# Gated linear attention with 26 of its projection tiles computed in pairs, by seven products of quarters, and with x kept in DRAM meanwhile

## Chip, cores and metric

The kernel runs on one core of one Trainium2 chip, in one launch. The metric is the device time of a run in microseconds (us). Before the change the median of 3 runs is 1719.75 us (1718.37 to 1721.04).

## What is computed

The program is a whole model on 512 tokens with 1024 channels: a first block (convolution, attention, feed-forward), and a second with a layer of gated linear attention and one of sparse attention. Only the gated-attention layer changes:

```python
def gla_mixer(x, w_in, w_a2, b_a, gn_g, w_out):
    h = x @ w_in                              # q, k, v, z, a side by side
    ...
    g = jax.nn.log_sigmoid((a @ w_a2 + b_a).astype(jnp.float32)) / GLA_GATE_NORM
    ...
    q_t = q * (GLA_DK ** -0.5) * jnp.exp(G)
    k_t = k * jnp.exp(-G)
    ...
    o = o * lax.rsqrt(jnp.mean(o * o, axis=-1, keepdims=True) + NORM_EPS)
    o = o.reshape(B, L, D_INNER) * gn_g
    return (o.astype(x.dtype) * jax.nn.silu(z)) @ w_out
...
x = layer_norm(ALPHA * x + y, ln_g[i], ln_b[i])
```

There are 4 heads. Of each, queries and keys are 2 x 256 channels and the gate z has 512, so q, k and z together are 8 tiles of 128 channels a head, each of them 1024 x 128 weights times x.

## The kernel before

All tensors are held with channels on the 128 partitions and the 512 tokens along the free axis. Precision comes from splitting: a float32 operand is held as a high and a low part (`XH`, `XL` for x, `whi`, `wlo` for weights), and a product of two is three matmuls (high times high, high times low, low times high). `split` makes them: a copy on ACT (the high part), then a subtraction on DVE (the low part). Every call of an engine through a helper is recorded on L112.

One projection tile (`proj` and `part`, L237 to L252) loads 1024 x 128 weights by one DMA on SP's queue (`slab`, a `raw` buffer of 4), splits them in two halves of 128 x 512 (8 buffers of `whi` and 8 of `wlo`), and runs 8 steps of three 512-column matmuls, 24 in all, into one PSUM bank (`bank("mm")`, three of them in turn). Then the bank is read once: a copy to `gqk` for a tile of queries or keys (`gla_qk`), Silu to `gz` for a gate (`gla_z`), both on ACT.

The main loop (L1310 to L1362) goes over the heads h. Ahead of it stand the decay, the scaling and `gla_v` (values) of head 0. In a head PE's order is: four steps of scores (`gla_scores`, L1266), four z tiles among them, four steps of weighted values (`gla_av`, with `weighted` at L487 and L489), the decay of the next head (`gla_decay`: two matmuls of 256 columns, then on ACT Abs, exp and Ln with a load of the function table ahead of a change of function, and on DVE `gs`), the four tiles of queries and keys of the next head, the norm (`gla_norm`: DVE multiplies `gz` by the norm that PE spread into `ps_t`, L396, and splits the result), the eight output tiles of the head (`w_out`: DVE adds each to `X`), with the exponentials of the next head (`gla_exp`), and the values of the next head (`gla_v`).

PE's order is that of the program, by hand. ACT, DVE, POOL and SP each run one queue in the order in which a scheduler placed them; weight loads and splits are placed ahead of their use (`AHEAD`). Each queue runs in order: an instruction that waits holds all behind it.

Of the kernel before, what the change touches and what calls it, by code (L numbers as in the profile page):

```python
# [92 lines left out]
def program(tc, a, out, upto=99):  # L93
# [107 lines left out]
    class Folded:  # L201
# [20 lines left out]
        def part(self, ps, xs, k0, k1, cs):  # L222
            n = len(xs)
            for k in range(k0, k1):
# [68 lines left out]
    X = cp.tile([128, DC, S], F32, name="X")  # L293
# [310 lines left out]
    for c in range(DC):  # L604
        acc.add_square(X[:, c, :])

    pos1, T1 = tmp("pos1"), sp.tile([128, S], F32, name="T1", bufs=1)
    dve.tensor_copy(pos1, posi)
    angles(T1, pos1, 0)

# [494 lines left out]

    WO = {}

    def w_out(name, grp, i, ts, sums=None, cs=FULL):
# [51 lines left out]
    jp = gq.tile([128, 128], F32, name="jp")  # L1160
# [84 lines left out]
    def gla_z(h, i):  # L1245
# [59 lines left out]
    gla_z(0, 0)  # L1305
    for b in range(NB):
        gla_v(0, b, (lambda: None, lambda: gla_exp(0, 0), lambda: gla_exp(0, 1), lambda: None)[b])
    gla_z(0, 1)
    for h in range(4):
        gla_scores(h, 0)  # L1310
# [450 lines left out]
```

## Time and profile before

| | |
|---|---|
| median of 3 runs | 1719.75 us (1718.37 to 1721.04) |
| profiled execution: time, span | 1719.7 us, 1718.0 us |
| PE busy | 1704.8 us, 99% of the span |
| DVE, ACT, POOL busy | 1197.1, 870.9, 70.3 us (70%, 51%, 4%) |
| mean granted TensorE clock | 0.998 |
| the gated-attention layer | about 812 to 1195 us of the span |

"Busy" counts the time in which an engine has an instruction under way. A matmul's row gives its start and a length; matmuls overlap, so what one costs is read from the distance of two starts. "idle before" names who ended the idle time ahead of an instruction. The granted clock is that of TensorE, 1.00 being 2.4 GHz and 0.50 being 1.2 GHz.

### The profile page before, as it was taken

Reading aid. Unit: us, or ns where it says so; the run is one execution under the profiler, and the core shown is the slowest. Engines: PE = TensorE matmul, PEld = TensorE weight load, DVE = VectorE, ACT = ScalarE, POOL = GpSimd, SP = SyncE. Lnnn points to the kernel's source line nnn. Section 1 sums busy time; section 2 is a strip of 40 time slices with the busy share of each in tenths; the row PEclk is TensorE's granted clock in tenths of the full one; section 3 lists DMA queues with packets and bytes.
Section 4 is the critical chain, followed back from the end, with each engine's and each line's share of the span. In section 5 each row is a group of like instructions: output and inputs, shape, how many; then the busy total and the mean of one; then the engine's idle time right before and its main releaser. Section 6 shows DMA issues by size and latency. Waiting matters only on the chain.

```text
span 1718.0 us, 23818 instructions
## 1 busy us (share of the span) xinstructions
PE 1704.8 (99%) x8815; PEld 1453.1 (85%) x8815; DVE 1197.1 (70%) x2604; ACT 870.9 (51%) x1642; POOL 70.3 (4%) x98
## 2 busy tenths in 40 slices
PE   9999999999999999999999999999999999999999
PEld 7788888898888888899888888888988888888898
DVE  8788545389727657688545473546879987888886
ACT  7466433365434434455753644533765356444554
POOL 2244000000000000000000000000000000000000
PEclk9999999999999999999999999999999999999999
DMA  6232332223333232333312322224232232121231
GB/s 217 86 99 74 123 98 98 86 76 111 96 98 95 80 115 85 98 123 125 104 60 70 102 83 86 74 86 135 85 125 74 87 98 62 62 75 62 68 105 62
DMA packets 51188, 161.11 MB, mean 94 GB/s; under 512 B 6144, under 2 KB 7552, under 8 KB 51072
## 3 DMA queue, kind: packets, MB, share of 16 engines
q1 hardware_dynamic: 49968, 157.82, 28.7%
q0 software_dynamic: 960, 1.57, 0.4%
q8 instruction: 69, 1.13, 0.3%
q14 instruction: 47, 0.39, 0.1%
q10 hardware_dynamic: 144, 0.20, 0.0%
HBM read 153.28 MB, written 4.72 MB: 92 GB/s over the span
## 4 chain that ended last, share of the span: by engine, by line
PE 94%; DVE 3%; ACT 2%; issue 1%; DMA 0%; POOL 0%; SPq 0%; ACTq 0%; DVEq 0%
PE ps_mm L246 71%; PE ps_s L246 7%; PE ps_o L487 2%; PE ps_mm L273 2%; PE ps_mm L274 2%; PE ps_mm L272 2%; PE ps_t L505 1%; PE ps_s L272 1%; PE ps_t L1266 1%; PE ps_s L274 1%; PE ps_s L273 1%; PE ps_t L396 1%; PE ps_s L487 1%; DVE wlo L112 0%; PE ps_s L1204 0%
## 5 line engine op out<-in xcount | busy, mean ns | idle before, releaser
L112 ACT ACTIVATE whi<-raw 128x512 fp32r<-128x512 f32 (+1 forms) x550 | 336.8, 621 | 433.8 <-PE ps_mm L246 375.9
L246 PE MATMUL ps_mm<-XH,wlo 128*128 128x512 f32 (+1 forms) x1381 | 516.9, 374 | 0.3 <-DVE up L112 0.3
L246 PE MATMUL ps_mm<-XH,whi 128*128 128x512 f32 (+1 forms) x1381 | 515.3, 373 | 0.0
L246 PE MATMUL ps_mm<-XL,whi 128*128 128x512 f32 (+1 forms) x1381 | 514.6, 373 | 0.0
L112 DVE TENSOR_TENSOR wlo<-raw,whi 128x512 fp32r<-128x512 f32 (+2 forms) x547 | 368.1, 683 | 167.0 <-ACT whi L112 165.1
L246 PEld LDWEIGHTS ps_mm<-XH,wlo 128*128 128x128 f32 x1381 | 260.4, 189 | 45.7 <-DVE wlo L112 0.8
L246 PEld LDWEIGHTS ps_mm<-XL,whi 128*128 128x128 f32 x1381 | 260.4, 189 | 45.7 <-DVE XL L112 0.2
L246 PEld LDWEIGHTS ps_mm<-XH,whi 128*128 128x128 f32 x1381 | 260.6, 189 | 44.0 <-ACT whi L112 0.4
L112 DVE SCALAR_TENSOR_TENSOR upt<-up,vec,upt 128x511 f32<-128x511 f32 (+1 forms) x88 | 65.4, 750 | 10.7 <-ACT upt L112 9.5
L112 ACT ACT_TABLE_LOAD x47 | 60.3, 1283 | 6.8 <-issue 2.1
L246 PE MATMUL ps_mm<-fh,wlo 128*128 128x512 f32 (+1 forms) x153 | 55.7, 364 | 0.0
L246 PE MATMUL ps_mm<-fl,whi 128*128 128x512 f32 (+1 forms) x153 | 55.6, 363 | 0.0
L246 PE MATMUL ps_mm<-fh,whi 128*128 128x512 f32 (+1 forms) x153 | 55.6, 363 | 0.0
L272 PE MATMUL ps_mm<-whi,XH 128*128 128x512 f32 x128 | 50.2, 392 | 0.4 <-ACT whi L112 0.4
L273 PE MATMUL ps_mm<-wlo,XH 128*128 128x512 f32 x128 | 50.0, 390 | 0.3 <-DVE wlo L112 0.3
L274 PE MATMUL ps_mm<-whi,XL 128*128 128x512 f32 x128 | 49.9, 390 | 0.0
L246 PE MATMUL ps_mm<-pthi,wlo 128*128 128x512 f32 (+1 forms) x128 | 48.7, 381 | 0.0
L112 DVE TENSOR_TENSOR up<-ps_mm,RU 128x512 f32<-128x512 f32 x41 | 28.2, 691 | 29.0 <-PE ps_mm L246 29.0
L246 PE MATMUL ps_mm<-ptlo,whi 128*128 128x512 f32 (+1 forms) x128 | 48.0, 375 | 0.4 <-DVE ptlo L112 0.2
L246 PE MATMUL ps_mm<-dth,wlo 128*128 128x512 f32 (+1 forms) x128 | 48.1, 376 | 0.0
L246 PE MATMUL ps_s<-XL,whi 128*128 128x256 f32 (+1 forms) x160 | 47.5, 297 | 0.6 <-DVE XL L112 0.6
L246 PE MATMUL ps_mm<-dtl,whi 128*128 128x512 f32 (+1 forms) x128 | 48.1, 375 | 0.0
(546 smaller groups left out, 3163.0 us busy)
## 6 DMA issues: line engine op xcount, KB each, us to landing
raw<-in_w_ffn_up SPq DMA_DIRECT2D x44, 512.0 KB, 3.5
raw<-in_dsa_w SPq DMA_DIRECT2D x38, 512.0 KB, 3.5
raw<-in_w_in SPq DMA_DIRECT2D x31, 512.0 KB, 3.3
raw<-in_gla_qk SPq DMA_DIRECT2D x16, 512.0 KB, 4.1
raw<-in_gla_z SPq DMA_DIRECT2D x16, 512.0 KB, 3.5
raw<-in_gla_v SPq DMA_DIRECT2D x16, 512.0 KB, 3.4
raw<-in_gla_w_out SPq DMA_DIRECT2D x16, 512.0 KB, 3.5
raw<-in_ple_gate_w SPq DMA_DIRECT2D x16, 512.0 KB, 3.5
```

The costliest lines, as they stand in the source:

```text
L112: r = f(*args, **kw).ins
L246: pe.matmul(ps[:m, cs], l_, r_, start=(k == 0 and i == 0), stop=(k == n - 1 and i == 2))
L272: pe.matmul(ps, lh, rh, start=(i == 0), stop=False)
L273: pe.matmul(ps, lh, rl, start=False, stop=False)
L274: pe.matmul(ps, ll, rh, start=False, stop=(i == n - 1))
L396: pe.matmul(ps[:, b * 128:(b + 1) * 128], r.to_broadcast([128, 128]), ident, start=True, stop=True)
L487: pe.matmul(ps[:m, c0:], vs[j][a_], r[b_], start=(j == 0 and i == 0), stop=(j == NB - 1 and i == 2))
L505: pe.transpose(ps[:, j * 128:(j + 1) * 128], p_[:, j * 128:(j + 1) * 128], ident)
L1266: pe.matmul(ps_[:, bi], l_, r_, start=(c == 0), stop=(c == 1))
```

## The change

Two tiles of 128 channels become one `Pair`. Its weights are a 2 x 2 block: a, b the two halves of the first tile's 1024 rows, c, d those of the second; x is a 2 x 2 block too (its lower and upper 512 channels, by the first and the last 256 tokens). Seven products of quarters replace eight. POOL makes four sums of the weights' quarters (128 x 512 each); seven parts are split on ACT and DVE instead of four. A product is 4 steps of three 256-column matmuls, so a pair has 84 of 256 columns where two tiles had 48 of 512. The seven accumulate into halves of two banks b0 and b1 of "mm": products 0, 2 and 4 into the first half of b0 (each on top of the one before), product 1 into its second half; 3 and 6 into the first half of b1, 5 into its second half. After products 0, 2 and 4 ACT copies the half bank to `kept`; after 1, 4, 5 and 6 DVE adds a half bank and a half of `kept` to the output.

Thirteen pairs are made: the first two z tiles of heads 1 to 3, the last two z tiles of all four heads, and both pairs of queries and keys of heads 1 to 3. `x_forms` makes the four sums of x's quarters once, in `gla_v` of head 0: 8 operations on POOL, 8 copies on ACT, 8 subtractions on DVE (`TH`, and `XT`, which takes `X`'s place). `X` is stored to DRAM (`XD`, eight DMAs of 256 KB); the output tiles of heads 0 to 2 inside the loop load their x tile into `xio` (two buffers), add, and store it; at head 3 x comes back by eight loads. `X` becomes tiles of two chunks (class `Chunks`, left out below); `gs` has one buffer instead of two.

```diff
+    class Pair:
+        def __init__(self, ap0, ap1):
...
+            (a_, b_), (c_, d_) = ((t_[:, :S], t_[:, S:]) for t_ in raw)
+            self.todo, self.parts = [a_, b_, a_, c_, tmp("s1"), b_, d_], []
+            with tc.high_priority(offset=AHEAD):
+                gps.tensor_tensor(self.todo[4], c_, d_, op=OP.add)
+                self.split(2)
+                gps.tensor_tensor(c_, a_, c_, op=OP.subtract)
+                gps.tensor_tensor(a_, self.todo[4], a_, op=OP.subtract)
+                gps.tensor_tensor(b_, b_, a_, op=OP.subtract)
...
+            def product(n):
+                if n == 0:
+                    st["b"] = bank("mm"), bank("mm")
+                b0, b1 = st["b"]
+                self.split(1)
+                ps = (b0[:, lo_], b0[:, hi_], b0[:, lo_], b1[:, lo_], b0[:, lo_], b1[:, hi_], b1[:, lo_])[n]
+                hi, lo = self.parts[n]
+                xs_ = quarters[n]
+                for k in range(4):
+                    th, tl = xs_[k]
+                    kc = slice(k * 128, k * 128 + 128)
+                    for i, (l_, r_) in enumerate(((hi, th), (hi, tl), (lo, th))):
+                        pe.matmul(ps, l_[:, kc], r_, start=(n in (0, 3) and k == 0 and i == 0),
+                                  stop=(k == 3 and i == 2), skip_group_check=n not in (0, 3))
...
+                if n in (0, 2, 4):
+                    copy(k1 if n == 2 else k0, ps, scale=scale)
+                if n == 1:
+                    sum_(o0[:, lo_], ps, k0)
+                elif n == 4:
+                    sum_(o1[:, hi_], b1[:, lo_], k0)
+                elif n == 5:
+                    sum_(o0[:, hi_], ps, k0)
+                elif n == 6:
+                    sum_(o1[:, lo_], ps, k1)
+                    done()
...
+        if away:
+            x_ = gp.tile([128, S], F32, name="xio", tag="xio", bufs=2)
+            with tc.high_priority(offset=AHEAD):
+                nc.sync.dma_start(x_, away[i])
...
+        if away:
+            nc.sync.dma_start(away[i], x_)
...
+    def gla_z_pair(h, i):
...
+        return Stream(pair.steps(x_quarters(), (two[:, 0, :], two[:, 1, :]), kept,
+                                 done=lambda: act.activation(two, two, AF.Silu)))
...
         gla_scores(h, 1)
         if h:
-            gla_z(h, 0)
+            z01.run(4)
         gla_scores(h, 2)
         gla_scores(h, 3)
+        z23 = gla_z_pair(h, 2)
         if h:
-            gla_z(h, 1)
+            z01.drain()
         if h < 3:
             gla_decay(h + 1, 0)
-        gla_z(h, 2)
+        z23.run(4)
+        if h < 3:
+            qk01 = gla_qk_pair(h + 1, 0)
         gla_av(h, 0)
-        gla_z(h, 3)
+        z23.drain()
...
             gla_av(h, 2)
-            gla_qk(h + 1, 0)
+            qk01.run(4)
+            qk23 = gla_qk_pair(h + 1, 2)
             gla_av(h, 3)
-            gla_qk(h + 1, 1)
+            qk01.drain()
             r = rms(GACC[h], 512, LN_EPS, "rg")
-            gla_qk(h + 1, 2)
+            qk23.run(4)
             gla_norm(h, spread(r))
-            gla_qk(h + 1, 3)
+            qk23.drain()
```

So the loop runs products 0 to 3 of a pair, then a step of other work (scores, weighted values, the spread of the norm), then products 4 to 6.

The compiled orders show how the parts stand to each other. First PE, at the turn from the second to the third z tile of head 1, with the decay between them (`W`, `AS`); before:

```order
L246 MATMUL ps_mm<-XH,whi 128x512
L246 MATMUL ps_mm<-XL,whi 128x512
L1178 MATMUL ps_s<-W_7609,AS 128x256 [waits PE_49]
L1178 MATMUL ps_s<-W_7609,AS 128x256
L246 MATMUL ps_mm<-XH,wlo 128x512 [waits DVE_49,Activation_49]
L246 MATMUL ps_mm<-XH,whi 128x512
```

After the change, on PE, the end of product 4 and the start of product 5 of that head's first z pair:

```order
L278 MATMUL ps_mm<-TH,whi 128x256
L278 MATMUL ps_mm<-XT_7898,whi 128x256
L278 MATMUL ps_mm<-TH,wlo 128x256
L278 MATMUL ps_mm<-XH,whi 128x256 [waits DVE_49]
L278 MATMUL ps_mm<-XL,whi 128x256
L278 MATMUL ps_mm<-XH,wlo 128x256
```

A tile had its waits (for its bank and its split weights) at its first matmuls. In a pair, product 1 waits for ACT's copy of product 0, product 2 for DVE's sum of product 1, product 4 for the copy of product 2, product 5 for DVE's sum behind product 4 (here), and product 6 for DVE's sum of product 5. The waits hold a bank as a whole, although the halves differ.

Next ACT, at the same turn: the end of z's first pair and the start of the second. `ge` is the decay's Abs, exp and Ln. Before, in head 0:

```order
L112 ACTIVATE ge<-ge 128x512 [waits Activation_49]
L112 ACTIVATE whi<-raw 128x512 [waits DMAHW0_49,PE_49]
L112 ACT_TABLE_LOAD
L112 ACTIVATE ge<-ge 128x512 [waits Activation_49]
L112 ACT_TABLE_LOAD
L112 ACTIVATE gz<-ps_mm 128x512 [waits PE_49]
```

And after the change, on ACT, at that turn in head 1:

```order
L112 ACTIVATE whi<-raw 128x512 [waits PE_49]
L112 ACTIVATE ge<-ps_s 128x512 [waits PE_49]
L112 ACT_TABLE_LOAD
L112 ACTIVATE gz<-gz 128x1024 [waits DVE_49]
L112 ACT_TABLE_LOAD
L112 ACTIVATE ge<-ge 128x512 [waits Activation_49]
L112 ACTIVATE kept<-ps_mm 128x256 [waits PE_49]
L112 ACT_TABLE_LOAD
L112 ACTIVATE ge<-ge 128x512 [waits Activation_49]
```

The copy to `kept` behind product 0 of the second pair stands behind the decay's Abs, Silu of both tiles of the first pair, two loads of the table and the decay's exp; a third load and Ln follow it.

Last DVE, at the norm of a head, among the products of the second pair of queries and keys. Before:

```order
L112 TENSOR_TENSOR gz<-ps_t,gz 128x512 [waits PE_49]
L112 TENSOR_TENSOR gz<-ps_t,gz 128x512 x2
L112 TENSOR_TENSOR ptlo<-gz,pthi 128x512 [waits Activation_49] x3
L112 TENSOR_TENSOR gz<-ps_t,gz 128x512
L112 TENSOR_TENSOR wlo<-raw,whi 128x512
```

And after the change, on DVE, there:

```order
L112 TENSOR_TENSOR gz<-ps_t,gz 128x512 [waits PE_49]
L112 TENSOR_TENSOR gz<-ps_t,gz 128x512 x2
L112 TENSOR_TENSOR ptlo<-gz,pthi 128x512 [waits Activation_49] x2
L112 TENSOR_TENSOR gz<-ps_t,gz 128x512
L112 TENSOR_TENSOR ptlo<-gz,pthi 128x512 [waits Activation_49]
L112 SCALAR_TENSOR_TENSOR gqk<-ps_mm,kept 128x256
L112 TENSOR_TENSOR ptlo<-gz,pthi 128x512 [waits Activation_49]
```

The sum behind product 4, for which product 5 waits, stands behind seven operations of the norm; before, nothing that PE's next matmuls needed stood there.

## Rows read from the trace of the kernel before

**Rows 1.** The page, part 4: the chain that ended last, by engine.

```profile
PE 94%; DVE 3%; ACT 2%; issue 1%; DMA 0%; POOL 0%; SPq 0%; ACTq 0%; DVEq 0%
```

**Rows 2.** Busy time by engine and granted clock, the gated-attention layer.

```profile
812.00:1195.00 383.00, 381.71 (x1870) 321.05 (x1869) 203.93 (x407) 192.16 (x303) 0.96 (x3) 1.00 0.27 87
```

**Rows 3.** Timeline of PE (start, length): first and last matmul of a z tile.

```profile
848.32 0.39 PE L246 MATMUL ps_mm<-XH,wlo 128*128 128x512 f32 x1
...
853.53 0.40 PE L246 MATMUL ps_mm<-XL,whi 128*128 128x512 f32 x1
```

**Rows 4.** Timeline of PE: 256-column matmuls, first and last of 24.

```profile
798.60 0.28 PE L246 MATMUL ps_mm<-XH,wlo 128*128 128x256 f32 x1
...
801.36 0.28 PE L246 MATMUL ps_mm<-XL,whi 128*128 128x256 f32 x1
```

**Rows 5.** Timeline of all engines: a split that PE waits for.

```profile
828.00 0.61 ACT L112 ACTIVATE whi<-raw 128x512 fp32r<-128x512 f32 x1
...
828.67 0.50 PE L272 MATMUL ps_mm<-whi,XH 128*128 128x512 f32 x1 [0.37 <-ACT whi L112]
...
828.74 0.68 DVE L112 TENSOR_TENSOR wlo<-raw,whi 128x512 fp32r<-128x512 f32 x1
...
829.48 0.50 PE L273 MATMUL ps_mm<-wlo,XH 128*128 128x512 f32 x1 [0.30 <-DVE wlo L112]
...
829.82 0.40 PE L274 MATMUL ps_mm<-whi,XL 128*128 128x512 f32 x1
```

**Rows 6.** Timeline: scores end on PE, DVE reads them.

```profile
832.83 1.05 PE L1204 MATMUL ps_s<-dec,gs 128*128 128x128 f32 x8
...
833.92 0.17 DVE L112 COPY ends<-ps_s 128x8 f32<-128x8 f32 x1 [2.18 <-PE ps_s L1204]
```

**Rows 7.** Groups by shape, ACT, whole run (busy us, mean ns).

```profile
L112 ACT ACTIVATE whi<-raw 128x512 fp32r<-128x512 f32 x513 | 318.6, 630 | 400.6 <-PE ps_mm L246 348.3 <-PE ps_s L246 23.7 <-issue 20.8
L112 ACT ACT_TABLE_LOAD x47 | 60.3, 1283 | 6.8 <-issue 2.1 <-PE ps_s L246 1.6 <-PEq L1752 1.2
...
L112 ACT ACTIVATE pthi<-ps_t 128x256 fp32r<-128x256 f32 x28 | 10.6, 377 | 0.2 <-PE ps_t L505 0.2
...
L112 ACT ACTIVATE ex<-ex 128x1024 f32<-128x1024 f32 x8 | 8.4, 1050 | 0.0
```

**Rows 8.** Groups by shape, DVE, whole run.

```profile
L112 DVE TENSOR_TENSOR wlo<-raw,whi 128x512 fp32r<-128x512 f32 x513 | 350.1, 692 | 165.4 <-ACT whi L112 163.5
...
L112 DVE SCALAR_TENSOR_TENSOR pn<-Ee,vec,ps_t 128x256 f32<-128x256 f32 x16 | 7.6, 475 | 0.0
```

**Rows 9.** Timeline of DVE: the norm of head 0 (`gla_norm`).

```profile
895.21 1.89 DVE L112 TENSOR_TENSOR gz<-ps_t,gz 128x512 f32<-128x512 f32 x3 [2.25 <-PE ps_t L396]
897.01 1.89 DVE L112 TENSOR_TENSOR ptlo<-gz,pthi 128x512 fp32r<-128x512 f32 x3
898.81 0.69 DVE L112 TENSOR_TENSOR gz<-ps_t,gz 128x512 f32<-128x512 f32 x1
```

**Rows 10.** Busy time by engine and granted clock, around an idle PE.

```profile
79.00:80.00 1.00, 0.00 (x0) 0.00 (x0) 0.31 (x2) 0.66 (x2) 0.91 (x2) 1.00 0.62 239
...
82.00:83.00 1.00, 1.00 (x6) 1.00 (x6) 0.31 (x2) 0.61 (x2) 0.95 (x1) 0.50 0.30 98
```

**Rows 11.** Timeline of PE there: the idle time, and 512-column matmuls behind it.

```profile
81.01 0.66 PE L505 MATMUL ps_t<-con,p 128*128 128x128 f32 x2 [2.65 <-ACT p L112]
...
82.75 0.63 PE L246 MATMUL ps_mm<-XH,whi 128*128 128x512 f32 x1
83.17 0.63 PE L246 MATMUL ps_mm<-XL,whi 128*128 128x512 f32 x1
```

**Rows 12.** Timeline of POOL and of DVE: one sum each, at one time.

```profile
67.61 1.61 POOL L695 TENSOR_TENSOR ac<-ac,rub 128x512 f32<-128x512 f32 x1 [7.81 <-DVE ac L112]
...
67.97 2.40 DVE L112 TENSOR_TENSOR wlo<-raw,whi 128x512 fp32r<-128x512 f32 x2
```

**Rows 13.** The page, part 6: issue to landing.

```profile
Ee<-e2d SPq DMA_DIRECT2D x7, 256.0 KB, 4.7
```

More of the change, by code (lines that the diff above doesn't have):

```diff
@@ L229, in part, with split, steps, sum_ @@
                     pe.matmul(o_, w_, x_[:, cs], start=(k == 0 and i == 0), stop=(k == n - 1 and i == 1))
+    class Pair:
+        def __init__(self, ap0, ap1):
+            with tc.high_priority(offset=AHEAD):
+                raw = []
+                for ap in (ap0, ap1):
+                    raw.append(wp.tile([128, 1024], F32, name="raw", tag="raw", bufs=4))
+                    nc.sync.dma_start(raw[-1], ap)
+            (a_, b_), (c_, d_) = ((t_[:, :S], t_[:, S:]) for t_ in raw)
[6 more added lines that the diff above has]
+                gps.tensor_tensor(b_, b_, a_, op=OP.subtract)
+        def split(self, n):
+            for _ in range(n if len(self.parts) < 7 else 0):
+                with tc.high_priority(offset=AHEAD):
+                    hi = wp.tile([128, 512], F32R, name="whi", tag="whi", bufs=WBUFS)
+                    lo = wp.tile([128, 512], F32R, name="wlo", tag="wlo", bufs=WBUFS)
+                    split(hi, lo, self.todo[len(self.parts)])
+                    self.parts.append((hi, lo))
+        def steps(self, quarters, outs, kept, scale=1.0, done=lambda: None):
+            st = {}
+            o0, o1 = outs
+            lo_, hi_ = HALVES
+            def product(n):
[12 more added lines that the diff above has]
+                                  stop=(k == 3 and i == 2), skip_group_check=n not in (0, 3))
+                def sum_(o_, ps_, kept_):
+                    dve.scalar_tensor_tensor(o_, ps_, scale, kept_, op0=OP.mult, op1=OP.add)
+                k0, k1 = kept[:, lo_], kept[:, hi_]
+                if n in (0, 2, 4):
[9 more added lines that the diff above has]
+                    done()
+            return [lambda n=n: product(n) for n in range(7)]
@@ L292, in program, with __init__, __getitem__ @@
     xin, w_in = a["xT"], a["w_in"]
-    X = cp.tile([128, DC, S], F32, name="X")
+    class Chunks:
+        def __init__(self, name, dt=F32):
+            self.name, self.dt, self.tiles = name, dt, {}
+        def __getitem__(self, at):
+            p_, c, cs = at
+            c0, n = (c.start, c.stop - c.start) if isinstance(c, slice) else (c, 1)
+            i = c0 // 2
+            if i not in self.tiles:
+                self.tiles[i] = cp.tile([128, 2, S], self.dt, name=f"{self.name}{i}", tag=f"X{i}", bufs=1)
+            return self.tiles[i][p_, slice(c0 % 2, c0 % 2 + n) if isinstance(c, slice) else c % 2, cs]
+    X = Chunks("X")
     g_first = cp.tile([128, DC], F32, name="g_first")
@@ L605, in program @@
         acc.add_square(X[:, c, :])
-    pos1, T1 = tmp("pos1"), sp.tile([128, S], F32, name="T1", bufs=1)
+    pos1, T1 = tmp("pos1"), ap_.tile([128, S], F32, name="T1")
     dve.tensor_copy(pos1, posi)
@@ L1106, in program, with w_out @@
     WO = {}
-    def w_out(name, grp, i, ts, sums=None, cs=FULL):
+    def w_out(name, grp, i, ts, sums=None, cs=FULL, away=None):
         key = name, 4 * grp + i // 2
@@ L1169, in program, with x_forms, form, quarter @@
     GS, EX, VS, ZS, PTS, TS, QKS, GACC, VW = ({} for _ in range(9))
+    XT = Chunks("XT", F32R)
+    XD = [drp.tile([128, S], F32, name=f"xd{i}", bufs=1) for i in range(DC)]
+    for i in range(DC):
+        nc.sync.dma_start(XD[i], X[:, i, :])
+    TH = gq.tile([128, 4, 4, 256], F32R, name="TH")
+    kept = gq.tile([128, S], F32, name="kept")
+    def x_forms(p):
+        two = lambda x: x.rearrange("p (a b) -> p a b", b=256)
+        b11, b12, b21, b22 = (X[:, 4 * i + 2 * p:4 * i + 2 * p + 2, cs] for i in range(2) for cs in HALVES)
+        ts = [tmp("form") for _ in range(4)]
+        t1, t2, t3, t4 = (two(t_[:, :]) for t_ in ts)
+        gps.tensor_tensor(t1, b12, b11, op=OP.subtract)
+        gps.tensor_tensor(t2, b22, t1, op=OP.subtract)
+        gps.tensor_tensor(t3, b22, b12, op=OP.subtract)
+        gps.tensor_tensor(t4, b21, t2, op=OP.subtract)
+        for f, t_ in enumerate(ts):
+            hi = TH[:, f, 2 * p:2 * p + 2, :]
+            copy(hi, two(t_[:, :]))
+            sub(two(XT[:, (0, 1, 4, 5)[f] + 2 * p, :]), two(t_[:, :]), f32v(hi))
+    def form(f):
+        return [(TH[:, f, k, :], XT[:, (0, 1, 4, 5)[f] + k // 2 * 2, k % 2 * 256:k % 2 * 256 + 256])
+                for k in range(4)]
+    def quarter(i, cs):
+        return [(XH[:, 4 * i + k, cs], XL[:, 4 * i + k, cs]) for k in range(4)]
+    def x_quarters():
+        return (quarter(0, HALVES[0]), quarter(1, HALVES[0]), form(1), form(2), form(0), quarter(1, HALVES[1]),
+                form(3))
     def gla_decay(h, i):
         if i == 0:
-            GS[h] = ga.tile([128, NB, 256], F32, name="gs", tag="gs", bufs=2)
+            GS[h] = ga.tile([128, NB, 256], F32, name="gs", tag="gs", bufs=1)
         ps_, e_ = bank("s"), tmp("ge")
@@ L1249, in gla_z, with gla_qk_pair @@
         act.activation(ZS[h][:, i, :], ps_, AF.Silu)
+    def gla_z_pair(h, i):
+        if i == 0:
+            ZS[h] = gp.tile([128, 4, S], F32, name="gz", tag="gz")
+        pair = Pair(a["gla_z"][4 * h + i], a["gla_z"][4 * h + i + 1])
+        two = ZS[h][:, i:i + 2, :]
+        return Stream(pair.steps(x_quarters(), (two[:, 0, :], two[:, 1, :]), kept,
+                                 done=lambda: act.activation(two, two, AF.Silu)))
+    def gla_qk_pair(h, j):
+        pair = Pair(a["gla_qk"][4 * h + j], a["gla_qk"][4 * h + j + 1])
+        for i in (j, j + 1):
+            QKS[h, i] = ga.tile([128, S], F32, name="gqk", tag="gqk", bufs=4)
+        return Stream(pair.steps(x_quarters(), (QKS[h, j], QKS[h, j + 1]), kept, 1.0 / 16 if j < 2 else 1.0))
     def gla_scores(h, j):
```

17 lines of the change are left out of this document (13 added, 4 removed).

## The prediction

> **What bounds the kernel now.** I read the chain that ended last first: 94% of it is PE [rows 1]. Then the windows: in the gated-attention layer (812 to 1195 us) PE is busy for 381.71 of 383 us at a granted clock of 1.00, while ACT has 192.16 us of work and DVE 203.93 us [rows 2]. So PE never waits to speak of, and the reader should see two things: time saved on PE is saved in the end, and so is time in which PE is made to stand still. The other engines have about half of the layer free, so what they do costs nothing by its sum. It costs only where PE stands until one of them has finished. The question is therefore not how many columns a pair has but what each product waits for.
>
> **What the pairs save.** From the first to the last matmul of a z tile are 23 starts in 853.53 - 848.32 = 5.21 us [rows 3], 0.2267 us for 512 columns. Matmuls of 256 columns start (801.36 - 798.60) / 23 = 0.120 us apart [rows 4]. A pair took 48 x 0.2267 = 10.88 us and takes 84 x 0.120 = 10.08 us: **-0.80 us**, and 13 x 0.80 = -10.4 us for all. Half the columns cost 0.53 of the time, so the seven eighths of the columns become 0.93 of the time.
>
> **What each product waits for.** By the compiled order, four times in a pair PE needs a result that can only begin when its own last matmul is out. The prices:
> - A 256-column matmul lasts 0.28 us where the next would start after 0.12 [rows 4]: 0.16 us until the product is in the bank.
> - A step from engine to engine: 0.04 us from PE to DVE (832.83 + 1.05 to 833.92) [rows 6], 0.06 us from ACT to PE (828.00 + 0.61 to 828.67) and from DVE to PE (828.74 + 0.68 to 829.48) [rows 5]. From PE to ACT and from ACT to DVE I take 0.03.
> - ACT's copy of 128x256 out of PSUM 0.38 us [rows 7]; DVE's sum of that shape with a factor 0.475 us [rows 8].
> - The first matmul after an idle time: the next starts 829.82 - 829.48 = 0.34 us later instead of 0.227 [rows 5], so 0.1 us each.
>
> With ACT and DVE free, PE stands for 0.16 + 0.03 + 0.38 + 0.06 = 0.63 us ahead of product 1; 0.16 + 0.04 + 0.475 + 0.06 = 0.74, and 0.1 for the start, 0.84 ahead of products 2 and 6; 0.16 + 0.03 + 0.38 + 0.03 + 0.475 + 0.06 = 1.13 ahead of product 5, whose sum needs a copy first. Product 4's wait has other work of PE in front and costs nothing; product 3 has none. Together 0.63 + 2 x 0.84 + 1.13 = 3.44 us, and with the slow starts not yet counted 3.6, so a pair costs at least 3.6 - 0.8 = **+2.8 us**, and 13 of them +36 us.
>
> **What stands in front of those copies and sums.** ACT and DVE run in order, so I add what the orders show ahead of each:
> - A split ahead of the copy behind product 0. It waits for a weight buffer that product 0 itself reads, so it cannot begin earlier: 0.62 us on ACT [rows 7]. This holds for the first z pair and the second pair of queries and keys: 0.63 + 0.62 = 1.25.
> - A split around product 4, freed by product 4 too: copy 0.62, then 0.03, DVE's subtraction 0.69 [rows 8], the sum 0.475 and 0.06: 1.87 instead of 1.13. This holds for all but one kind below.
> - The decay's chain on ACT ahead of the second z pair's first copy. After the first pair's product 6: a split (until 0.73 us), Abs 0.6, a table load 1.28, Silu of 128x1024 1.05, a table load 1.28, exp 0.63, the copy 0.38, the step 0.06, by rows of the same shapes [rows 7]: about 6.05 us, in which PE has the decay and product 0, 0.24 + 1.44 = 1.68 us. PE stands for 4.4 us. Then come a table load, Ln, `gs` (0.69), a subtraction (0.6) and the sum ahead of product 2, 3.7 us against 1.55: 2.15. In heads 1 and 2 a second z pair thus costs 4.4 + 2.15 + 1.87 + 0.84 - 0.8 = +8.4.
> - Head 0 has no Silu before it: 1.7 for the first wait, +5.8. Head 3 has no decay but the Silu: 2.1, then 0.84, 1.87, 0.84, less 0.8: +4.8.
> - The first pair of queries and keys has the second decay ahead of product 1 in the same way, with the Silu long over: 1.7 + 2.15 + 1.87 + 0.84 - 0.8 = +5.8.
> - The second has the norm on DVE ahead of the sum of product 4. From the first multiplication to the fourth's end it took 899.50 - 895.21 = 4.3 us [rows 9], and one more subtraction and the sum come after; from that 5.3 to 5.4 us, product 4 covers 1.44: 4.0. So 1.25 + 0.84 + 4.0 + 0.84 - 0.8 = +6.1.
> - The first z pair: 1.25 + 0.84 + 1.87 + 0.84 - 0.8 = +4.0.
>
> Sum: 3 x 4.0 + 2 x 8.4 + 5.8 + 4.8 + 3 x 5.8 + 3 x 6.1 = **+75 us**.
>
> **The rest.** `x_forms` gives DVE 8 x 0.69 = 5.5 us and ACT 8 x 0.62 = 5 us in `gla_v` of head 0, where both are half idle [rows 2]: 0, at most 5.5. The 20 output tiles of heads 0 to 2 that go by DRAM wait for loads of 256 KB, of which one took 4.7 us to land [rows 13], with two `xio` in turn; DVE holds only the bank's release, and three banks and the following 22 us of values give slack: 0, at most one such latency a head, 3 x 4.7 = 14. The eight loads at head 3 are issued ahead of two steps of values: 0, at most 4.7. One buffer of `gs` makes a decay wait for the exponentials of a head before, which end long ahead: 0. POOL's 52 sums run ahead with the weight loads.
>
> A subtraction on DVE that ran beside a sum on POOL did not proceed: two took 2.40 us [rows 12], where three took 1.89 [rows 9], so 1.1 us were lost while POOL worked until 69.22. The Trainium skill, SBUF — State Buffer, section "SBUF: two separate sides", calls the shared port an exclusive lock: of a DVE operation with two SBUF inputs and a GpSimd one, the loser blocks for the whole instruction. By that rule each of a pair's four sums can hold a split that stands in the path, and the trace agrees with its 2.40 us. In the sum by rows I take one such loss in every third pair, 13 / 3 x 1.1 = +5 at most, +2 taken.
>
> A pause also slows PE. After 2.65 us of idling the next 512-column matmuls started 83.17 - 82.75 = 0.42 us apart [rows 11], and the granted clock was 0.50 there, 1.2 GHz, after 1.00 before [rows 10]. From 81.01 to 83.80 at least, 2.8 us, PE ran at half speed: 1.4 us lost. Only two second z pairs and three second pairs of queries and keys have pauses of 4 us; in the former the following wait covers most. I take 3 x 1.4 = +4.
>
> **Sum:** 1719.7 (the profiled execution, the median's 1719.75) + 75 + 2 + 4 = about **1800 us**.
>
> **Rivals.**
> 1. Only the least waits (chance 0.13): splits, decay and norm finish earlier than their place tells, since every pause of PE gives ACT and DVE time. For it speaks their half-empty layer [rows 2]; against it that the splits are freed by the very product whose result is waited for, and that Silu needs the sum of product 6. 1719.7 + 36 = 1756, with half of the extras 1775.
> 2. The clock stays low (0.17): pauses of 1.9 and 2.2 us throttle too, since a pair's pauses follow each other at 1.5 to 3 us. One loss of 1.4 us a pair gives 1800 - 4 + 13 x 1.4 = 1814; two give 1832. The Trainium skill, TensorE: Matmul & The Clock Gate, section "HAM oscillation — how this bites in real kernels", tells of a kernel in which every burst behind a wait starts cold. By that rule the case of two losses a pair holds, 1832; the trace has one such place [rows 10], and it agrees.
> 3. The waits do not bite (0.04): PE streams through the products as through two tiles, because copies and sums of a half bank end beside the next half's matmuls. Then -10.4 and the time is 1709. It decides if the four pauses in a pair together stay below 0.80 us, 0.2 us each. Against it: the shortest copy alone takes 0.38 us [rows 7], and the orders show the waits.
> 4. The way of x by DRAM costs its bound of 14 (0.03), because the output tiles' additions hold their banks until a load has landed: 1814. Against it: SP has 22 us of values between two heads in which it only fetches weights.
>
> **How the numbers follow.** The forecast itself (1785 to 1808) has 0.62, rivals 1 to 4 what stands there. The range goes from the least waits, 1757, to two clock losses a pair and POOL's bound, 1832 + 3 = 1835. A measurement of this kernel tells 0.2%, 3.4 us, from no change. Faster is rival 3 with 0.04; the same needs stalls that by chance equal the gain, 0.01; slower 0.95.
>
> **What would show it.** In the profile after, the stretch of the layer is 455 to 475 us instead of 383, with PE busy for about 385 us of it. The waits of PE name ACT's `kept` (most of it, 13 x about 2) and DVE's sums on L278; the longest, about 4 us, are the second z pairs' of heads 1 and 2, and those behind the norm. 84 matmuls of a pair that start 0.12 us apart show the gain. The rest of the program keeps its time. The prediction is wrong if the sum of PE's waits on L278 is under 30 us, or if the time is lost in `w_out` behind DMAs, or in rows of 0.21 us for 256 columns at a clock of 0.50.

## The result, and the profile after

The changed kernel takes 1823.9 us (median of 6 runs, 1820.68 to 1825.19) against 1719.5 us: a ratio of 1.0604, 95% interval 1.059 to 1.0618. Its profiled span is 1822.2 us, 104.2 us longer than before. The forecast was 1800 us in a range of 1757 to 1835: the sign and the mechanism of the waits held, and the time is 24 us above.

The windows, cut ahead of the layer and behind it (columns: stretch and its length, then busy us and count of PE, PE's weight loads, DVE, ACT, POOL, then the granted clock, DMA share, GB/s):

```profile
0.00:812.00 812.00, 805.30 (x4091) 681.21 (x4092) 554.01 (x1063) 398.81 (x735) 69.94 (x92) 1.00 0.34 107
812.00:1300.00 488.00, 408.09 (x2339) 359.30 (x2338) 273.81 (x510) 222.13 (x371) 83.36 (x61) 0.94 0.29 94
1300.00:1822.00 522.00, 516.91 (x2856) 450.38 (x2854) 439.76 (x1132) 280.30 (x605) 2.77 (x5) 1.00 0.26 82
```

All of it is in the layer: about 488 us where 383 stood [rows 2]. PE stands idle for 80 of them, and is also busy for 26 us more (408 us; the forecast had said about 385). Most of that second part was not forecast. The waits of PE (us in total, times, longest) tell what ended the idle part:

```profile
PE ps_mm L278 <- ACT kept L112: 26.9, 13, 4.0
PE ps_mm L278 <- DVE gqk L112: 26.4, 18, 3.6
PE ps_mm L278 <- DVE gz L112: 20.8, 21, 1.7
PE ps_mm L314 <- DVE wlo L112: 3.7, 1, 3.7
```

The first three are the 13 x 4 = 52 waits inside pairs: 74.1 us. The fourth is one wait in head 0, which will matter below. Where before PE ran through two z tiles without a break [rows 3], a pair now reads like this one, the first z pair of head 1 (timeline of all engines: start, length; in brackets the idle time before and who ended it):

```profile
978.23 1.68 POOL L248 TENSOR_TENSOR raw<-s,raw 128x512 f32<-128x512 f32 x1 [3.04 <-DVE wlo L112]
...
979.35 0.71 DVE L112 TENSOR_TENSOR ptlo<-diag,pthi 128x128 fp32r<-128x128 f32 x1 [0.38 <-ACT pthi L112]
...
979.63 0.28 PE L278 MATMUL ps_mm<-XH,wlo 128*128 128x256 f32 x1
979.98 0.55 DVE L112 TENSOR_TENSOR ptlo<-ps_t,pthi 128x384 fp32r<-128x384 f32 x1
...
980.45 0.29 DVE L112 COPY_PREDICATED diag<-upper,ps_t 128x128 f32<-128x128 uint32 x1
980.77 0.31 ACT L112 ACTIVATE pthi<-diag 128x128 fp32r<-128x128 f32 x1 [1.07 <-DVE diag L112]
...
981.25 0.62 ACT L112 ACTIVATE whi<-raw 128x512 fp32r<-128x512 f32 x1
...
981.76 0.37 ACT L112 ACTIVATE kept<-ps_mm 128x256 f32<-128x256 f32 x1
...
982.19 0.58 PE L278 MATMUL ps_mm<-XH,whi 128*128 128x256 f32 x1 [2.28 <-ACT kept L112]
...
982.57 0.42 PE L278 MATMUL ps_mm<-XL,whi 128*128 128x256 f32 x1
...
982.79 0.41 PE L278 MATMUL ps_mm<-XH,wlo 128*128 128x256 f32 x1
...
985.71 0.39 PE L278 MATMUL ps_mm<-TH,whi 128*128 128x256 f32 x1 [0.59 <-DVE gz L112]
...
993.27 0.38 PE L278 MATMUL ps_mm<-XH,whi 128*128 128x256 f32 x1 [1.72 <-DVE gz L112]
993.49 0.28 PE L278 MATMUL ps_mm<-XL,whi 128*128 128x256 f32 x1
993.61 0.28 PE L278 MATMUL ps_mm<-XH,wlo 128*128 128x256 f32 x1
...
995.47 0.38 PE L278 MATMUL ps_mm<-TH,whi 128*128 128x256 f32 x1 [0.52 <-DVE gz L112]
```

The reader sees three things. The four waits stand ahead of products 1, 2, 5 and 6, as the compiled order said: 2.28, 0.59, 1.72, 0.52. The first is longer than its own copy explains: ACT idles 1.07 us for DVE, and DVE's small subtraction at 979.35 takes 0.71 us beside a sum on POOL, where one of that shape takes 0.29 in the kernel before. And behind that first wait the matmuls start 0.22 us apart, where behind 993.27 they start 0.12 apart.

The decay's chain, by ACT's rows between the two z pairs of head 1, and PE behind it:

```profile
997.60 0.58 ACT L112 ACTIVATE ge<-ps_s 128x512 f32<-128x512 f32 x1
...
998.20 1.28 ACT L112 ACT_TABLE_LOAD   x1
...
999.49 1.06 ACT L112 ACTIVATE gz<-gz 128x1024 f32<-128x1024 f32 x1
1000.57 1.28 ACT L112 ACT_TABLE_LOAD   x1
1001.86 0.63 ACT L112 ACTIVATE ge<-ge 128x512 f32<-128x512 f32 x1
1002.40 0.37 ACT L112 ACTIVATE kept<-ps_mm 128x256 f32<-128x256 f32 x1
...
1002.81 0.58 PE L278 MATMUL ps_mm<-XH,whi 128*128 128x256 f32 x1 [4.00 <-ACT kept L112]
1003.19 0.41 PE L278 MATMUL ps_mm<-XL,whi 128*128 128x256 f32 x1
1003.41 0.41 PE L278 MATMUL ps_mm<-XH,wlo 128*128 128x256 f32 x1
```

This is the forecast's chain, operation for operation. Windows of 1 us (columns as above) show the clock ahead of it, behind it, and once recovered:

```profile
996.00:997.00 1.00, 1.00 (x11) 1.00 (x10) 0.23 (x1) 0.00 (x0) 0.63 (x1) 1.00 0.00 0
...
1003.00:1004.00 1.00, 1.00 (x5) 1.00 (x6) 0.00 (x0) 1.00 (x1) 0.00 (x0) 0.50 0.00 0
...
1007.00:1008.00 1.00, 1.00 (x11) 1.00 (x10) 0.00 (x0) 0.00 (x0) 0.00 (x0) 1.00 0.71 172
```

**Theory after the result.** The bank-wide waits make the loss, 74 us of it directly; the 24 us above the forecast are mostly PE at 1.2 GHz behind pauses. Rivals: the loss lies in the rest of the change (x by DRAM, `x_forms`); or it lies in the chains of ACT and DVE and not in the banks; or POOL's lock on DVE makes the pauses.

### The profile page after: what moved, and what is told of

It reads as the page before. It is cut to its first block, busy times and chain, and to the rows that moved or that the text cites. A ratio compares the mean times of both kernels' runs of the same rounds, so it can differ in the third digit from the quotient of the medians.

```text
span 1822.2 us, 25220 instructions
## 1 busy us (share of the span) xinstructions
PE 1730.3 (95%) x9283; PEld 1490.9 (82%) x9283; DVE 1267.6 (70%) x2703; ACT 901.2 (49%) x1709; POOL 156.1 (9%) x158
## 5 line engine op out<-in xcount | busy, mean ns | idle before, releaser
L112 ACT ACTIVATE whi<-raw 128x512 fp32r<-128x512 f32 (+2 forms) x576 | 351.7, 621 | 519.8 <-PE ps_mm L314 357.0
L314 PE MATMUL ps_mm<-XH,wlo 128*128 128x512 f32 (+1 forms) x1173 | 434.7, 371 | 4.0 <-DVE wlo L112 3.7
L314 PE MATMUL ps_mm<-XH,whi 128*128 128x512 f32 (+1 forms) x1173 | 435.0, 371 | 0.0
L314 PE MATMUL ps_mm<-XL,whi 128*128 128x512 f32 (+1 forms) x1173 | 434.1, 370 | 0.0
L314 PEld LDWEIGHTS ps_mm<-XH,wlo 128*128 128x128 f32 x1173 | 221.7, 189 | 42.8 <-DVE wlo L112 4.8
L278 PE MATMUL ps_mm<-XH,whi 128*128 128x256 f32 x156 | 51.0, 327 | 54.8 <-ACT kept L112 26.9
L278 PE MATMUL ps_mm<-TH,whi 128*128 128x256 f32 x208 | 68.6, 330 | 19.4 <-DVE gqk L112 10.6
L278 PEld LDWEIGHTS ps_mm<-TH,whi 128*128 128x128 f32 x208 | 45.5, 219 | 25.4 <-DVE gqk L112 13.3
L278 PE MATMUL ps_mm<-TH,wlo 128*128 128x256 f32 x208 | 64.3, 309 | 0.0
L278 PE MATMUL ps_mm<-XT,whi 128*128 128x256 f32 x208 | 64.2, 309 | 0.0
```

The source lines that it names most:

```text
L112: r = f(*args, **kw).ins
L278: pe.matmul(ps, l_[:, kc], r_, start=(n in (0, 3) and k == 0 and i == 0), stop=(k == 3 and i == 2), skip_group_check=n not in (0, 3))
L314: pe.matmul(ps[:m, cs], l_, r_, start=(k == 0 and i == 0), stop=(k == n - 1 and i == 2))
```

## The experiments

Ratios are to the kernel before, run beside each.

**1. Fill the pauses.** Matmuls of 512 columns whose result nobody reads go into the third bank ahead of products 1, 2, 5 and 6, in such a number that they about fill each pause.

```diff
+                    st["idle"] = bank("mm")
+                for _ in range(fills[(1, 2, 5, 6).index(n)] if n in (1, 2, 5, 6) else 0):
+                    pe.matmul(st["idle"], XH[:, 0, 0:128], XH[:, 0, :], start=True, stop=True)
```

> The changed kernel with 512-column matmuls that nobody reads, into the third bank of mm, put ahead of products 1, 2, 5 and 6, about as many as fit into the pause there (0.227 us each). Every wait of a product stays. Theory: of the 104 us that the change lost, 74 are pauses on L278 and about 24 are TensorE at 0.50 behind the pauses. Then the granted clock of the layer goes from 0.94 to 0.99 or 1.00 and the time falls by 18 to 26 us, to 1798 to 1806. Rival: the 24 us more of PE busy time come from 256-column products that are slower as such (POOL or DVE beside them, weight loads); then the time stays at 1824, or rises by what the extra matmuls overrun.

1805.69 us, ratio 1.0501 (1.0483 to 1.0518), 18.2 us less than the change. The layer's window and PE's waits:

```profile
812.00:1283.00 471.00, 448.56 (x2603) 382.81 (x2602) 271.68 (x510) 223.18 (x373) 83.87 (x61) 0.99 0.31 98
```

```profile
PE ps_mm L281 <- DVE gz L112: 7.9, 18, 1.4
PE ps_mm L281 <- DVE gqk L112: 4.6, 15, 0.4
...
PE ps_mm L281 <- ACT kept L112: 3.0, 12, 0.4
```

PE does 262 matmuls more and the kernel is faster. The products still wait for the same copies and sums: the idle time left, 15.5 us, and 262 x 0.2267 = 59.4 us of filling make 74.9 us, where 74.1 were idle before. So 18 us is what the low clock costs. Starts on a pair's line that are 0.18 to 0.25 us apart, those right behind a wait left out, fell from 216 to 28; at 45.8 / 216 - 0.118 = 0.094 us each that is 17.7 us, which agrees.

**2. The rest of the change without pairs.** Plain tiles in the pairs' places; `x_forms`, x in DRAM and `xio` stay.

```diff
-        pair = Pair(a["gla_z"][4 * h + i], a["gla_z"][4 * h + i + 1])
...
+        return Stream([lambda: gla_z(h, i)] + [lambda: None] * 3 + [lambda: gla_z(h, i + 1)])
```

> The changed kernel with each pair computed as two plain tiles again, at the places of before; x in DRAM, the sums of x's quarters (their results unused), one gs buffer and the rest of the change stay. Theory: the rest costs only the pause of 3.7 us ahead of the second z tile of head 0 and about 1.3 us of clock behind it: 1723 to 1726. Rival: the way of x through DRAM costs 14 us or more under w_out: 1733 or more.

1721.7 us, ratio 1.0016 (1.0006 to 1.0025), 1.3 us below its range: head 0's wait is 1.5 us here and not 3.7. The way by DRAM and the forms together cost 2.4 us; that rival falls.

**3. Three banks a pair.** Products 0, 2, 4 in one bank, 3 and 6 in the second, 1 and 5 in the third, in the order 0, 3, 1, 2, 5, 4, 6, so that a bank is read while another is written; the break for other work comes ahead of the last.

```diff
+                n = (0, 3, 1, 2, 5, 4, 6)[at]
...
-                ps = (b0[:, lo_], b0[:, hi_], b0[:, lo_], b1[:, lo_], b0[:, lo_], b1[:, hi_], b1[:, lo_])[n]
+                ps = (b0[:, lo_], b2[:, lo_], b0[:, lo_], b1[:, lo_], b0[:, lo_], b2[:, hi_], b1[:, lo_])[n]
```

> The changed kernel with three banks a pair and the products in the order 0, 3, 1, 2, 5, 4, 6 (products 1 and 5 in a bank of their own), six of them ahead of the other work in between: every copy and sum has at least one product in front of who waits for it. Theory: the pauses are those of a bank held by a copy or sum, so nearly all go; what stays is ACT's chain of decay, Silu and table loads in front of the first copy of the second z pair (about 4.6 us in two heads, 2 us in three pairs of queries and keys) and 5 us in head 0: 1720 to 1742. Rival: it is the splits on ACT and DVE and POOL's sums that limit a pair, not the banks; then pauses of the same length stand before other products and the time stays over 1790.

1756.47 us, ratio 1.0218 (1.0201 to 1.0235):

```profile
PE ps_mm L281 <- ACT kept L112: 17.9, 12, 4.1
...
PE ps_mm L281 <- DVE gqk L112: 2.3, 3, 0.8
PE ps_mm L281 <- DVE gz L112: 2.2, 3, 0.9
```

The pauses fell from 74.1 to 22.4 us and the time by 67: handing a bank over between products that follow each other makes two thirds of the loss. The edit changes the third bank, the order and the break at once, and no run separates them. The expectation had counted the chains on ACT that still hold copies (the longest are the second z pairs', 4.13 us each in heads 1 and 2); above its 1742 the time stays also by waits outside the pairs (3.4 us for the norm's split results) and by 85 starts on the pairs' line that are 0.18 to 0.25 us apart.

**4. With three banks, the decays behind a pair's sixth product.**

```diff
             z01.run(6)
+        if h < 3:
+            gla_decay(h + 1, 0)
...
-        if h < 3:
-            gla_decay(h + 1, 0)
```

> As e3_three_banks, and both decays of a head are issued behind a pair's sixth product instead of ahead of the next pair, so that Abs, exp, Ln and their table loads no longer stand in front of a first copy. Theory: another 8 to 15 us less than e3_three_banks, 1710 to 1730; the columns saved (10.4 us) show only if what is left of pauses stays under 5 us. Rival: the table chain then stands in front of the next pair's splits and the pauses only move: within 4 us of e3_three_banks.

1764.27 us, ratio 1.0265 (1.0249 to 1.028): 8 us worse than experiment 3, outside both expectations. The wait moved to PE's sums of the norm's squares, which on ACT now stand behind the second decay's chain:

```profile
PE ps_t L443 <- DVE acc_o L112: 13.8, 4, 4.4
PE ps_mm L281 <- DVE gz L112: 7.8, 7, 1.7
PE ps_mm L281 <- ACT kept L112: 4.2, 3, 3.1
```

**5. With three banks, the decays a stage earlier,** among the values of the head before, `x_forms` two steps later, the norm behind the third product.

```diff
+                if h < 2 and b in (1, 2):
+                    gla_decay(h + 2, b - 1)
...
-            qk23.run(4)
+            qk23.run(3)
```

> As e3_three_banks, with the decays of a head issued a stage earlier, among the values of the head before (22 us without a pair), the sums of x's quarters after the second block of values instead of after the first, and the norm's spread behind the third product of the second pair of queries and keys. Theory: e3_three_banks has 22 us of pauses on L281, 3.7 in head 0 and about 12 us of clock behind them; with ACT's table chain gone from the pairs these fall to under 8 us, and the columns' 10.4 us show: 1709 to 1722. Rival: splits and POOL's lock take over (seven subtractions and four sums of POOL in a pair of 10 us); then pauses behind wlo or whi show and the time stays over 1735.

1742.21 us, ratio 1.0126 (1.0107 to 1.0144). The second z pairs' 4.13 us became 0.47, but 19.5 us of pauses remain, in other pairs (3.82 in head 0, 0.94, 0.8 and 1.72 in each first z pair of heads 1 and 2, 1.66 in each second pair of queries and keys). The time is in the rival's range, but the waits on the pairs' line name copies and sums, not splits.

**6. The same with priority for a pair's copies and sums,** and head 0's second decay behind the sixth product of its pair.

```diff
+                with tc.high_priority(offset=AHEAD):
+                    if n in (0, 2, 4):
+                        copy(k1 if n == 2 else k0, ps, scale=scale)
```

> As e5_three_banks_decay_early, with the copies and sums of a pair placed as far ahead as the splits are, and head 0's second decay behind the sixth product of its pair. Theory: of the 19.5 us of pauses on L281 the 3.8 of head 0 go, the rest stays where the next pair's splits stand in front of a copy: 1734 to 1742. Rival: the copies come forward everywhere and the pauses fall under 5 us: 1715 to 1728.

1741.33 us, ratio 1.013 (1.0116 to 1.0144): no gain over experiment 5, at the upper end of its theory's range. Head 0's 3.82 us are gone and the pauses are 15.7 us, but head 0's wait for a split grew from 2.6 to 3.6 us, and one of 1.4 us for `gs` is new. A higher rank alone doesn't free the copies; what holds them here stays open.

**7. The decays early, banks as in the change.**

```diff
-        if h < 3:
-            gla_decay(h + 1, 0)
...
+                if h < 2 and b in (1, 2):
+                    gla_decay(h + 2, b - 1)
```

> The changed kernel with two banks as it is, and only the decays issued a stage earlier, as in e5_three_banks_decay_early. Theory: the pauses ahead of products 1 and 2 of the second z pairs (4.0, 4.0, 3.2, 1.3 us) and of the first pairs of queries and keys (1.5 and 1.9 us, three times) fall to 0.5 to 1.1 us each; the pauses on L278 fall from 74 to 55 to 62 us and the low clock by a few stretches: 1796 to 1810. Rival: the decay chain is not what the copies waited for; then the time is within 5 us of 1824.

1815.05 us, ratio 1.0552 (1.0536 to 1.0568). It misses its range by 5 us: pauses of 67.7 us, 6 less, and head 0's wait for a split 2 us less. The decays' extras do go (in heads 1 and 2 the second z pairs' first wait falls from 4.00 to 1.8), but the first z pairs' first wait there grew from 2.28 to 3.54, and head 0's from 3.19 to 5.70. Of the two places tried for the chain with shared banks, each is ahead of some copy.

**8. Six pairs,** of the kinds that had room: the second z pairs and the first pairs of queries and keys of heads 1 to 3, with experiment 5's banks and decays; plain tiles elsewhere.

```diff
+        if h == 0 or i == 0:
+            return plain(gla_z, h, i)
...
+        if j:
+            return plain(gla_qk, h, j)
```

> As e5_three_banks_decay_early, with pairs only where that kernel has no pause over 0.5 us: the second z pair of heads 1 to 3 and the first pair of queries and keys of heads 1 to 3; the other seven are plain tiles again. Theory: 6 x 0.8 = 4.8 us of columns saved, less about 1.5 us of pauses, less 2.4 us that the rest of the change costs by e2_no_pairs and up to 2.6 us in head 0: 1715 to 1722, no difference or a little faster. Rival: next to plain tiles the pairs wait again: over 1726.

1721.29 us, ratio 1.0011 (1.0002 to 1.002). No wait over 0.1 us on a pair's line; what is left is one wait for a split in head 0, as in the change:

```profile
PE ps_mm L316 <- DVE wlo L112: 3.8, 2, 3.7
```

**9. The change without POOL's four sums of the weights.**

```diff
-            self.todo, self.parts = [a_, b_, a_, c_, tmp("s1"), b_, d_], []
+            self.todo, self.parts = [a_, b_, a_, c_, d_, b_, d_], []
...
-                gps.tensor_tensor(c_, a_, c_, op=OP.subtract)
-                gps.tensor_tensor(a_, self.todo[4], a_, op=OP.subtract)
```

The pairs then multiply other weights, in the same shapes. The run takes away two things at once: POOL beside DVE, and a split's wait for the sum that it splits.

> The changed kernel without POOL's four sums of weights a pair: parts 2 to 6 are split from the plain quarters, so the products of these parts are of other weights; all instructions of the other engines stay. Theory: POOL's lock on DVE and the late sums cost little, 0 to 5 us of the 104, since the pauses come from the banks: 1818 to 1825. Rival: subtractions that POOL blocks lengthen the pauses (1.1 us each, two in a pair): 1790 to 1810.

1813.42 us, ratio 1.0551 (1.0535 to 1.0568), 10.5 us less than the change, between the two expectations. The first z pair of head 1 has its first wait back at 0.94 us, and head 0's wait is 1.5 instead of 3.7. PE's rows of head 1, the first z pair's first wait, then the second pair's first two:

```profile
973.65 0.39 PE L274 MATMUL ps_mm<-XH,whi 128*128 128x256 f32 x1 [0.94 <-ACT kept L112]
...
993.05 0.39 PE L274 MATMUL ps_mm<-XH,whi 128*128 128x256 f32 x1 [4.00 <-ACT kept L112]
993.27 0.28 PE L274 MATMUL ps_mm<-XL,whi 128*128 128x256 f32 x1
993.39 0.27 PE L274 MATMUL ps_mm<-XH,wlo 128*128 128x256 f32 x1
...
994.38 0.42 PE L274 MATMUL ps_mm<-XL,whi 128*128 128x256 f32 x1
994.60 0.42 PE L274 MATMUL ps_mm<-XH,wlo 128*128 128x256 f32 x1
996.65 0.58 PE L274 MATMUL ps_mm<-TH,whi 128*128 128x256 f32 x1 [1.63 <-DVE gz L112]
```

The pauses fell by 74.1 - 70.4 = 3.7 us in total and head 0's wait by 2.2; slow starts fell from 216 to 194, 2 us. The remaining 2 or 3 us are not assigned.

**10. Six pairs, the forms of x later,** behind the values instead of among them, and behind both decays of head 1.

```diff
-        if b < 2:
-            x_forms(b)
...
+    x_forms(0)
+    x_forms(1)
```

> e8_six_pairs with the x_forms and the two decays of head 1 issued after both pairs of z tiles of head 0 that come first, so that ScalarE's two copies of x in transposed halves no longer stand ahead of head 0's exps. Theory: the 3.68 us wait of TensorE for the late weight split in head 0 goes, and with it about 1.3 us of low clock: 1714 to 1719, likeliest 1716.3, against 1721.3 of e8 and 1719.5 of the kernel before. Rival: the copies then stand ahead of the splits of head 0's later tiles and the wait only moves: 1720 or more.

1732.2 us, ratio 1.0068 (1.0055 to 1.0082), 11 us worse than experiment 8. The rival's outcome, but by another cause, which DVE's and POOL's rows show:

```profile
865.59 10.18 DVE L112 TENSOR_TENSOR XT<-form,TH 128x512 fp32r<-128x512 f32 x6
866.77 1.74 POOL L1278 TENSOR_TENSOR form<-X,X 128x512 f32<-128x512 f32 x1
...
868.48 1.74 POOL L1279 TENSOR_TENSOR form<-X,form 128x512 f32<-128x512 f32 x1
```

Six subtractions that alone take 0.69 us each [rows 8] take 10.18 us together, while POOL works from 865.20 to 875.23 with no gap over 0.08 us; they wait their turn, one by one. Behind them PE waits 8.8 us for parts of the scores; ahead of them it waits 3.2 us for `gs` of the moved decays. Where `x_forms` stands in the change, the same is seen more mildly:

```profile
832.83 6.39 DVE L112 TENSOR_TENSOR XT<-form,TH 128x512 fp32r<-128x512 f32 x5 [1.73 <-ACT TH L112]
833.67 1.61 POOL L1277 TENSOR_TENSOR form<-X,form 128x512 f32<-128x512 f32 x1 [1.20 <-DVE XT L112]
```

**11 and 12. Six pairs with POOL's sums on DVE:** first those of x alone, then those of the weights too.

```diff
-        gps.tensor_tensor(t1, b12, b11, op=OP.subtract)
+        dve.tensor_tensor(t1, b12, b11, op=OP.subtract)
...
-                gps.tensor_tensor(s1, c_, d_, op=OP.add)
+                dve.tensor_tensor(s1, c_, d_, op=OP.add)
```

> e8_six_pairs with the eight sums of x's quarters made by DVE instead of POOL. Theory: the 3.7 us wait of TensorE in head 0 is there because POOL's sums hold DVE's subtractions of x (832.83 to 839 us in the changed kernel: five in 6.39 us where they take 0.69 each); without POOL at that place DVE ends sooner, though it has 8 x 0.69 = 5.5 us more to do, and the wait falls below 2 us: 1717 to 1720, against 1721.3. Rival: it is the work ahead of head 0's exponentials itself that comes too late, or POOL's weight sums there: the wait stays at 3 us or more, 1720.5 to 1724.

> e12 with the four weight sums of each of the six pairs on DVE too, so that POOL does nothing in the layer: 24 x 0.69 = 16.6 us more on DVE, which has about 140 us free in the layer. Theory: no sum holds a split any more, the wait in head 0 is below 1.6 us as without pairs, no new wait on the pairs: 1714 to 1718, below the kernel before. Rival: DVE works in order, so a weight sum that waits for its DMA or for a split of its buffer holds the splits behind it, and TensorE waits for splits instead: 1720 or more.

The first: 1719.84 us, ratio 1.0 (0.9992 to 1.0009); its time is still in the theory's range, but its wait in head 0 is 3.3 us, so the theory of that wait falls and the rival's cause holds: three subtractions still take 3.71 us there, beside POOL's sums of weights. The second: 1717.0 us, ratio 0.9985 (0.9976 to 0.9994), in its theory's range and the only version faster than before, by 2.6 us in the medians; six pairs' columns alone would give 6 x 0.97 = 5.8. Busy time by engine over the whole run (share of the span, instructions), of the first:

```profile
PE 1702.9 (99%) x9031; PEld 1461.1 (85%) x9031; DVE 1241.7 (72%) x2662; ACT 883.0 (51%) x1672; POOL 104.7 (6%) x122
```

And of the second:

```profile
PE 1700.0 (99%) x9031; PEld 1459.0 (85%) x9031; DVE 1239.4 (72%) x2686; ACT 880.9 (51%) x1672; POOL 70.5 (4%) x98
```

In the second, DVE has 24 sums more, 24 x 0.69 = 16.6 us of work, and is busy for 2.3 us less: what it took over from POOL it had been losing to POOL. Head 0's wait falls to 1.46 us, as without pairs.

## Why the forecast held, and where it was off

The waits, forecast (each less 0.16 us of running out and, where charged, 0.1 of slow start, which the idle time in a row does not hold) and measured, in us:

| pair | product 1 | product 2 | product 5 | product 6 |
|---|---|---|---|---|
| first z, head 1 | 1.09, 2.28 | 0.58, 0.59 | 1.71, 1.72 | 0.58, 0.52 |
| second z, head 1 | 4.24, 4.00 | 1.99, 0.67 | 1.71, 1.72 | 0.58, 0.52 |
| second z, head 0 | 1.54, 3.19 | 1.99, 1.30 | 1.71, 1.72 | 0.58, 0.52 |
| second z, head 3 | 1.94, 1.83 | 0.58, 0.52 | 1.71, 1.67 | 0.58, 0.52 |
| first q and k, from head 0 | 1.54, 1.48 | 1.99, 1.91 | 1.71, 1.72 | 0.58, 0.52 |
| second q and k, from head 0 | 1.09, 0.88 | 0.58, 0.59 | 3.84, 3.56 | 0.58, 0.52 |

- **The waits: right.** Over the 13 pairs the forecast's terms make 75.3 us of idle time; measured are 74.1. That the totals are so near is in part luck: the first z pairs' first waits and head 0's are 3 x 1.19 + 1.65 = 5.2 us longer than forecast, the others 6.4 us shorter. Without POOL's sums (experiment 9) these first waits are 0.94 and 1.49, near the forecast's 1.09 and 1.54. Experiment 3 shows that most of the waits go when a bank is not handed over between neighbouring products. The Trainium skill, PSUM — Partial Sum Buffer, section "PSUM bank collisions raise a hardware error", says that two engines must not be in one bank at the same time, which gives the bank-wide wait a reason; no run here tried a pair without that wait.
- **The columns: right, a little better.** Starts on the pairs' line are 0.118 us apart at full clock (743 of them), so a pair gains 10.88 - 84 x 0.118 = 0.97 us instead of 0.80, 12.6 in all. (The forecast's 5.21 / 23 is 0.2265 and not 0.2267; that is 0.01 us a pair.) Against that every product behind a wait starts slowly (0.22 us to the next start instead of 0.12): 52 x 0.1 = 5.2 us, of which the sum had charged 2. With 52 x 0.16 = 8.3 us of running out: 74.1 + 8.3 + 5.2 - 12.6 = 75.0. It equals the forecast's +75 because the misses of its parts cancel.
- **The clock: the term that was mis-sized.** "I take 3 x 1.4 = +4." Measured: 18 us by experiment 1; 45.8 - 216 x 0.118 = 20.3 us by the rows, of which 22 starts of 0.20 us, the first of a product behind other work of PE, are no loss of the clock: 18.4. That is 14 of the 24 us above the forecast. The forecast charged only pauses of 4 us; those of about 2 us throttle too, as rival 2 says. Behind the 13 pauses of 1.83 us and more there are 12 stretches of slow starts, one in every pair but the first z pair of head 2, with some 16 starts of 0.21 us each; behind the 39 shorter pauses none begins. So this is rival 2 with one loss a pair; its other form, two losses a pair, is seen in none. 11 of the 52 products behind a wait are slow from their first starts on, as at 982.19, and six more fall to the low clock further in. The Trainium skill, TensorE: Matmul & The Clock Gate, section "HAM oscillation — how this bites in real kernels", tells of a kernel in which every burst behind a wait starts cold; the trace here disagrees for 41 of 52, whose waits are mostly shorter than those of that kernel.
- **POOL: too small.** +2 was taken and at most 5. Experiment 9 measured 10.5 us with all that follows: 1.3 us in each first z pair, 2.2 us in head 0's wait for a split, and clock. The sum had the lock hold a split beside it; what the rows from 979.35 to 982.19 show held is a whole chain, since ACT's next operations wait for DVE and the copy stands behind them in ACT's queue.
- **`x_forms`: within its bounds of 0 to 5.5,** where 0 was taken. Head 0's wait for a split is 3.7 us in the change. 1.5 us of it are there without any pair (experiment 2) and without POOL's sums of weights (experiments 9 and 12); the other 2.2 are POOL's, named above. No run leaves `x_forms` out, so that the 1.5 us are its own is likely and not shown.
- **x by DRAM: right, near 0.** Experiment 2, with all of it, is 2.4 us above before, 1.5 of them head 0's wait. In experiments 11 and 12 one wait of 1.1 us for `xio` shows.
- **The second z pair's product 2** was forecast at 1.99 and waits 0.67 us: product 1 ran at 1.2 GHz meanwhile (from 1002.81), so the chain behind `gs` had more time. A slower PE pays part of its wait. No run tests this by itself.

- **The signs.** The layer takes 488 us where 455 to 475 were forecast, and ACT's `kept` is not most of the waits: 26.9 of 74.1 us, where DVE's sums have 47.2. Of the signs of being wrong one is there in part: rows of 0.21 us at a clock of 0.50, with 18 us against 74 us of waits.

Sum: 75.0 + 20.3 + 3.7 = 99.0 of 104.2 us in the spans. Of the other 5 us most lie on the pairs' line too: from start to next start its matmuls take 240.3 us where 26 tiles took 26 x 24 x 0.2267 = 141.5, 98.9 more, and 75.0 + 20.3 explain 95.3 of these. The rest is not assigned.

## What to carry to other kernels

Here the fewer columns gained nothing, because most accumulations ended in a bank that the next one had to enter: count the handovers, price each by the copy or sum with what stands ahead of it in its queue, and give each running product a bank that nobody reads meanwhile. Then price the clock: idle time on PE is paid again in slow matmuls behind it, here about a quarter again (18 us on 74). And an elementwise sum handed to POOL to spare DVE may take from DVE as much as it spares.

## What the runs showed of the hardware

- The clock can fall some time behind the pause, and the length of one pause doesn't settle it. In experiment 9 the matmuls behind a pause of 4.00 us started 0.12 us apart at first and 0.22 apart about 1.3 us later (993.27 and 994.38), and the next product, behind 1.63 us, was slow from its first matmul (0.58 us long instead of 0.39). In the change 2.28 us were followed by 0.50 of full speed in head 1, and in head 2 they were not; in experiment 7 a pause of 1.72 us was followed by slow starts and one of 1.83 us was not.
- The lock between DVE and POOL is strict: back to back on both, six subtractions took 1.70 us each instead of 0.69, one for each sum of 1.59 to 1.74 us on POOL. The Trainium skill, SBUF — State Buffer, section "SBUF: two separate sides", says that the loser blocks for the whole instruction; these rows agree. With POOL's 24 sums of weights on DVE (experiment 12), DVE is busy for 2.3 us less, not 16.6 more.
